# Sixteen instead of twelve feature tiles of a SwiGLU's gate and up projections by seven block products

## The chip, the cores and the metric

The kernel runs on one core of a Trainium2 chip, as one launch. The metric is the device time of that launch in microseconds (us), lower is better. Engines are named as in the profile: PE (TensorE, matrix products; PEld is its weight load), DVE (VectorE), ACT (ScalarE), POOL (GpSimd) and SP, whose queue issues nearly all the DMAs here.

## The reference

A decoder trunk of two layers over 512 tokens with 1024 features, all in float32. Each layer is a SwiGLU half step, a mixing step with three attention branches, and a second SwiGLU half step. There are therefore four SwiGLU sub-layers, and the change touches these alone:

```python
def _swiglu(t, w_gate, w_up, w_down):
    return (jax.nn.silu(t @ w_gate) * (t @ w_up)) @ w_down

for l in range(DEPTH):                      # DEPTH = 2
    f = _swiglu(_rmsnorm(h, ffn1_pre_g[l]), ffn1_w_gate[l], ffn1_w_up[l], ffn1_w_down[l])
    h = h + 0.5 * _rmsnorm(f, ffn1_post_g[l])
    ...                                     # mixing step
    f = _swiglu(_rmsnorm(h, ffn2_pre_g[l]), ffn2_w_gate[l], ffn2_w_up[l], ffn2_w_down[l])
    h = h + 0.5 * _rmsnorm(f, ffn2_post_g[l])
```

The hidden width D_FF is 2816, that is 22 tiles of 128 features.

## The kernel before, in words

**Products.** Every float32 operand is split in two parts, `h` (rounded by a cast on ACT) and `l` (the rest, a subtraction on DVE), and a product is three matmuls, h·h, h·l and l·h (`mm3`, lines 214 to 216). Weights come in pieces ("units") of 128 x 1024 values, 512 KB each: SP issues the load into one of two `raw` buffers, ACT casts it to `wh`, DVE subtracts to `wl`; there are four `wh` and four `wl` buffers. A queue of jobs `Q` runs PE work in a written order and asks for the units of the coming jobs ahead (four units, which is two products).

**The four sub-layers** are named a0, c0, a1, c1 (`ffn`, called four times). Each has 22 feature tiles for gate and up, computed in three ways:

- *Halved pair.* The first pair of tiles runs in two halves of the tokens, since the second half of the tokens is still being normalised (`halved`).
- *Plain pair.* Two feature tiles, all 512 tokens: gate (`gates`), then up (`ups`), 2 x 2 x 8 x 3 = 96 matmuls of 128x512.
- *Group.* Four feature tiles, token-major (`group`, `gate_up`). The product of a 2x2 block matrix of the activations (token halves by input halves) and a 2x2 block matrix of the weights (input halves by gate | up) is made by seven block products instead of eight, each 4 x 2 x 3 = 24 matmuls of 128x512. Their left factors are sums of activation blocks (`sums`: the tiles `r` and, split, `ag` 2 to 5); their right factors are sums of weight blocks, made on DVE in the tiles `kt` (`BlockUnit.load`). After a group, 16 transposes of 128x128 on PE turn the result feature-major (`feature_major`, tiles `th`), and ACT copies it to `hr`.

**Accumulators.** Each of the seven products accumulates in a pair of PSUM banks. `SUM` says in which of three sums product n lies, and a sum that is read out goes on being added to:

```python
SUM = (0, 1, 2, 0, 2, 0, 0)
ORDER = (0, 2, 3, 4, 5, 1, 6)        # the order in which the products run
```

The tag `mm` has four banks, that is two pairs. With sum 0 kept throughout, sum 1 and sum 2 take turns at the other pair. The read-out of products 0, 2 and 3 is a copy on ACT, of product 6 the silu on ACT, of 1, 4 and 5 an addition on DVE (line 744).

**Down.** Sixteen feature tiles go through two sets of seven block products with the down weights (`products`, `downs(0)` and `downs(1)`), the last six tiles through plain products (`down`).

**Order before, in each sub-layer.** Halved pair (tiles 0, 1); plain pair 14 with the three steps of `sums` beside it; groups at 2, 6, 10, each one's transposes after two products of the next; then plain pairs 16, 18 and 20 woven with the two sets of down products: gates 16, transposes, ups 16, down 0 2 3, gates 18, down 4 5 1 6, ups 18, down 0 2 3, gates 20, down 4 5 1 6, ups 20.

A scheduler turns what is written into a fixed order for each engine before anything runs, and adds the semaphores; each engine then takes its instructions in that order.

Of the kernel before, what the change touches and what calls it, by code (L numbers as in the profile page):

```python
# [17 lines left out]
P = 128  # L18
# [4 lines left out]
def kernel(  # L23
# [611 lines left out]
    W_H, W_U = 4.8, (8.0, 7.0, 7.0, 5.7)  # L635


    TG = (2, 6, 10)

    HR = ("q", "q", "o", "o", "o", "tri", "tri", "rs")  # L640
    ORDER = (0, 2, 3, 4, 5, 1, 6)

    def ffn(l, src, wg, wu, wd, dst, name, spare, aside=None):

# [8 lines left out]
        def hidden(f, pg, pu):  # L653
            s = tmp(f"s{name}_{f}")
            nc.scalar.activation(s[:], pg[:], AF.Silu)
            if f < NC * FC:
                nc.vector.tensor_tensor(pair(f)[:, f % 2], pu[:], s[:], ALU.mult)
                return
            nc.vector.tensor_tensor(s[:], pu[:], s[:], ALU.mult)
            t = blk("q" if f >= 20 else "o", f"hid{name}_{f}")  # L660
            hid[f] = t[:, 0], t[:, 1]
            split(*hid[f], s[:])
            if f == NF - 1:
                tc.keep_in_program_order(nc.scalar.preload_act_table_set("natural_log_exp_and_others"))

        def pair(f):

            i = f // 2
            if i not in hr:
                hr[i] = stile([P, 2, S], HR[i], f"hr{name}_{i}", F32)  # L670
            return hr[i]
# [47 lines left out]
            t = st["ag", n]  # L719
            return t[:, 0, k, c], t[:, 1, k, c]  # L720

        def gate_up(f, n, uns):
# [12 lines left out]
            if n in (0, 2, 3, 6):  # L735
                st["c", i, j] = stile([P, 2, S], "f", f"c{name}_{f}_{i}{j}", F32)
            t = st["c", i, j]
            for e in range(2):
                if n == 6:
                    nc.scalar.activation(t[:, e], pts[e][:], AF.Silu)  # L740
                elif n in (0, 2, 3):
                    nc.scalar.copy(t[:, e], pts[e][:])
                else:
                    nc.vector.tensor_tensor(t[:, e], t[:, e], pts[e][:], ALU.add)
            if n == 1:
                nc.scalar.activation(t[:], t[:], AF.Silu)
            if n in (1, 6):
                u = st["c", i, 1]
                nc.vector.tensor_tensor(u[:], u[:], t[:], ALU.mult)
                st["hid", f, i] = u  # L750

        def feature_major(f):

            for i in range(2):
                u = st.pop(("hid", f, i))
                for b in range(2):
                    f2 = f + 2 * b
                    pt = pbank("z", f"th{name}_{f2}_{i}")
                    for m in range(2):
                        for e in range(2):  # L760
                            nc.tensor.transpose(pt[:, (2 * m + e) * P:(2 * m + e + 1) * P],
                                                u[:, e, (2 * b + m) * P:(2 * b + m + 1) * P], ident[:])
                    yield 0.45
                    out_ = pt[:].rearrange("p (m q) -> p m q", m=2)
                    nc.scalar.copy(pair(f2)[:, :, HALVES[i]], out_)

        def group(f):

            keep = Keep(lambda i, k0: stile([P, 2, S], "v", f"kt{name}_{f}_{i}_{k0}", F32)[:])
            for n in ORDER:  # L770
# [4 lines left out]
                yield uns, (lambda n=n, uns=uns: gate_up(f, n, uns))  # L775
            yield [], lambda: feature_major(f)

        def park():
# [5 lines left out]
        def halved(f, ug, uu, half):  # L784
            if half == 0:
                st["p"] = [pbank("mm", f"p{x}{name}_{f + m}") for x in "gu" for m in range(2)]
            else:
                Q.hold, Q.pinned = False, True
                Q.load_ahead()
                Q.pinned = False  # L790
            c = HALVES[half]

            for uns, pts in ((ug, st["p"][:2]), (uu, st["p"][2:])):
                for low in (False, True):
                    for un in uns:
                        for k, (m, pt) in itertools.product(range(un.nk), enumerate(pts)):
                            kk, cols = un.k0 + k, slice(m * P, (m + 1) * P)
                            wh, wl = un.h[:, k, cols], un.l[:, k, cols]
                            ah, al = act(kk, c)
                            if low:  # L800
                                nc.tensor.matmul(pt[:, c], wh, al, start=False, stop=False, skip_group_check=True)
                                nc.tensor.matmul(pt[:, c], wl, ah, start=False, stop=kk == ND - 1, skip_group_check=True)
                            else:
                                nc.tensor.matmul(pt[:, c], wh, ah, start=kk == 0, stop=False, skip_group_check=True)
                            yield (1 + low) * S // 2 * PE_US
            if half == 1:
                for m in range(2):
                    hidden(f + m, st["p"][m], st["p"][2 + m])
# [94 lines left out]
        def some(n):  # L903
            for one in itertools.islice(todo, n):
                Q.add(*one)

        def plain(f, *n):

            ug = wpair(wg[l], ND, f * P, f"g{name}_{f}")
            uu = wpair(wu[l], ND, f * P, f"u{name}_{f}")  # L910
            Q.add(ug, lambda: gates(f, ug))
            some(n[0])
            behind()
            Q.add(uu, lambda: ups(f, uu))
            some(n[1])

        def turns(f):
            *jobs, turn = group(f)
            later.append(turn)
# [3 lines left out]
            Q.add([], lambda: iter(first_factor(ci, 0) or ()))  # L923
            return products(ci)

        ug, uu = wpair(wg[l], ND, 0, f"g{name}_0"), wpair(wu[l], ND, 0, f"u{name}_0")
# [3 lines left out]
        Q.add(ug + uu, lambda: halved(0, ug, uu, 0), src.ready((0, 1)))  # L930
        Q.add([], lambda: halved(0, ug, uu, 1), src.ready(range(NT)))
        Q.add([], lambda: iter(park() or ()))
        marks["first"] = len(Q.jobs)
        summed = sums()
        todo = iter([([], lambda: iter(next(summed) or ()))] * 3)
# [4 lines left out]
        some(1)  # L940
        todo = turns(2)
        some(7)
        for g in (6, 10):
# [6 lines left out]
        todo = iter(())  # L950
        pairs = [(wpair(wg[l], ND, f * P, f"g{name}_{f}"), wpair(wu[l], ND, f * P, f"u{name}_{f}")) for f in (16, 18)]
# [11 lines left out]
        xg, xu = wpair(wg[l], ND, 20 * P, f"g{name}_20"), wpair(wu[l], ND, 20 * P, f"u{name}_20")  # L963
# [4 lines left out]
        Q.add(xu, lambda: ups(20, xu))  # L968
        if aside is not None:
            Q.add([], lambda: iter((next(norm),)))  # L970
        if aside is not None:
# [777 lines left out]
```

## Time and profile before

| | |
|---|---|
| three timed runs | 2387.38, 2388.46, 2388.64 us; median 2388.46 |
| span of the profiled execution | 2385.9 us |
| PE busy | 2374.6 us (100% of the span), 11720 matmuls in the trace |
| PEld, DVE, ACT, POOL busy | 84%, 77%, 55%, 3% |
| DMA | 337.13 MB, 141 GB/s in the mean |

The span runs from the first to the last instruction of one profiled execution, for which only the span is recorded; the timed runs lie 1.5 to 2.7 us above it. "Busy" is the time in which at least one instruction of the engine ran. A matmul row of 390 ns is one matmul from its start to its modelled end; the next one starts long before that, so rates are read from differences of start times.

### The profile page before, as it was taken

Reading aid. Unit: us, or ns where it says so; the run is one execution under the profiler, and the core shown is the slowest. Engines: PE = TensorE matmul, PEld = TensorE weight load, DVE = VectorE, ACT = ScalarE, POOL = GpSimd, SP = SyncE. Lnnn points to the kernel's source line nnn. Section 1 sums busy time; section 2 is a strip of 40 time slices with the busy share of each in tenths; the row PEclk is TensorE's granted clock in tenths of the full one; section 3 lists DMA queues with packets and bytes.
Section 4 is the critical chain, followed back from the end, with each engine's and each line's share of the span. In section 5 each row is a group of like instructions: output and inputs, shape, how many; then the busy total and the mean of one; then the engine's idle time right before and its main releaser. Section 6 shows DMA issues by size and latency. Waiting matters only on the chain.

```text
span 2385.9 us, 30907 instructions
## 1 busy us (share of the span) xinstructions
PE 2374.6 (100%) x11720; PEld 2009.0 (84%) x11720; DVE 1834.2 (77%) x2525; ACT 1317.5 (55%) x2136; POOL 74.0 (3%) x130
## 2 busy tenths in 40 slices
PE   9999999999999999999999999999999999999998
PEld 8888888888888898888898888888888888988887
DVE  7786877678777687778787878776787766778686
ACT  5655555677655554554545554556675655455443
POOL 0000000001110000000000000000001100000000
PEclk9999999999999999999999999999999999999999
DMA  5554664222323445545544536532232244445453
GB/s 188 166 174 136 202 212 151 71 76 76 89 67 120 150 133 177 168 150 194 185 142 159 185 133 231 184 115 80 63 89 80 73 139 142 159 142 185 141 203 124
DMA packets 234265, 337.13 MB, mean 141 GB/s; under 512 B 10346, under 2 KB 133506, under 8 KB 233604
## 3 DMA queue, kind: packets, MB, share of 16 engines
q1 hardware_dynamic: 234016, 335.13, 43.2%
q8 instruction: 92, 1.51, 0.3%
q14 instruction: 57, 0.47, 0.1%
q0 software_dynamic: 96, 0.03, 0.0%
q10 hardware_dynamic: 4, 0.00, 0.0%
HBM read 320.44 MB, written 14.68 MB: 140 GB/s over the span
## 4 chain that ended last, share of the span: by engine, by line
PE 95%; DVE 2%; DMA 1%; ACT 1%; issue 0%; DVEq 0%; ACTq 0%
PE pg L216 4%; PE pg L214 4%; PE pg L215 4%; PE pta L214 3%; PE pta L216 3%; PE pta L215 3%; PE pdc L214 3%; PE pdc L215 3%; PE pdc L216 3%; PE ptc L215 3%; PE ptc L216 3%; PE ptc L214 3%; PE pda L215 3%; PE pda L216 3%; PE pda L214 3%; PE pb L214 2%
## 5 line engine op out<-in xcount | busy, mean ns | idle before, releaser
L214 PE MATMUL pg<-us_a,wh_wg 128*128 128x512 f32 x384 | 151.0, 393 | 0.0
L216 PE MATMUL pg<-us_a,wl_wg 128*128 128x512 f32 x384 | 149.7, 390 | 0.0
L215 PE MATMUL pg<-us_a,wh_wg 128*128 128x512 f32 x384 | 149.6, 390 | 0.0
L188 ACT CAST wh_tc<-ktc 128x1024 fp32r<-128x1024 f32 x60 | 62.6, 1052 | 83.3 <-DVE ktc L349 37.2
L188 ACT CAST wh_ta<-kta 128x1024 fp32r<-128x1024 f32 x60 | 62.6, 1052 | 80.9 <-DVE kta L349 34.5
L189 DVE TENSOR_TENSOR wl_tc<-ktc,wh_tc 128x1024 fp32r<-128x1024 f32 x60 | 72.8, 1222 | 25.1 <-ACT wh_tc L188 24.9
L189 DVE TENSOR_TENSOR wl_ta<-kta,wh_ta 128x1024 fp32r<-128x1024 f32 x60 | 72.8, 1222 | 24.2 <-ACT wh_ta L188 23.9
L215 PE MATMUL pda<-wl_da,aha 128*128 128x512 f32 x224 | 87.1, 389 | 0.0
L216 PE MATMUL pda<-wh_da,ala 128*128 128x512 f32 x224 | 87.1, 389 | 0.0
L214 PE MATMUL pda<-wh_da,aha 128*128 128x512 f32 x224 | 87.1, 389 | 0.0
L215 PE MATMUL pdc<-wl_dc,ahc 128*128 128x512 f32 x224 | 87.1, 389 | 0.0
L214 PE MATMUL pdc<-wh_dc,ahc 128*128 128x512 f32 x224 | 87.1, 389 | 0.0
L216 PE MATMUL pdc<-wh_dc,alc 128*128 128x512 f32 x224 | 87.1, 389 | 0.0
L216 PEld LDWEIGHTS pg<-us_a,wl_wg 128*128 128x128 f32 x384 | 72.1, 188 | 15.2
L215 PEld LDWEIGHTS pg<-us_a,wh_wg 128*128 128x128 f32 x384 | 72.2, 188 | 14.1
L214 PEld LDWEIGHTS pg<-us_a,wh_wg 128*128 128x128 f32 x384 | 72.1, 188 | 14.1
L192 DVE SCALAR_TENSOR_TENSOR wl_wg<-raw_wg,wh_wg 128x1024 fp32r<-128x1024 f32 x48 | 58.6, 1220 | 25.9 <-ACT wh_wg L191 25.3
L214 PE MATMUL pta<-wh_ta,aga 128*128 128x512 f32 x192 | 75.1, 391 | 0.0
L214 PE MATMUL ptc<-wh_tc,agc 128*128 128x512 f32 x192 | 75.1, 391 | 0.0
L215 PE MATMUL ptc<-wl_tc,agc 128*128 128x512 f32 x192 | 74.8, 390 | 0.2 <-DVE wl_tc L189 0.2
L216 PE MATMUL pta<-wh_ta,aga 128*128 128x512 f32 x192 | 74.7, 389 | 0.0
L216 PE MATMUL ptc<-wh_tc,agc 128*128 128x512 f32 x192 | 74.7, 389 | 0.0
(536 smaller groups left out, 7675.8 us busy)
## 6 DMA issues: line engine op xcount, KB each, us to landing
raw_da<-in_ffn_w_down_dram SPq DMA_DIRECT2D x58, 512.0 KB, 3.7
raw_dc<-in_ffn_w_down_dram SPq DMA_DIRECT2D x58, 512.0 KB, 3.3
raw_ta<-in_ffn_w_gate_dram SPq DMA_DIRECT2D x48, 512.0 KB, 3.7
raw_wg<-in_w_gate_dram SPq DMA_DIRECT2D x48, 512.0 KB, 3.6
raw_tc<-in_ffn_w_gate_dram SPq DMA_DIRECT2D x48, 512.0 KB, 3.7
kta<-in_ffn_w_up_dram SPq DMA_DIRECT2D x24, 512.0 KB, 4.9
raw_wo<-in_w_out_dram SPq DMA_DIRECT2D x24, 512.0 KB, 3.3
ktc<-in_ffn_w_up_dram SPq DMA_DIRECT2D x24, 512.0 KB, 4.9
```

Of the source, the lines that this page charges most:

```text
L188: both = [nc.scalar.copy(h_ap, src)]
L189: make = lambda: nc.vector.tensor_tensor(l_ap, src, h_ap.bitcast(F32), ALU.subtract)
L192: make = lambda: nc.vector.scalar_tensor_tensor(l_ap, src, scale, h_ap.bitcast(F32), ALU.mult, ALU.subtract)
L214: nc.tensor.matmul(pt, lh, rh, start=start, stop=False, skip_group_check=free)
L215: nc.tensor.matmul(pt, lh, rl, start=False, stop=False, skip_group_check=free)
L216: nc.tensor.matmul(pt, ll, rh, start=False, stop=stop, skip_group_check=free)
```

## The change

Sixteen feature tiles go through groups, at 0, 4, 8 and 12, one after the other (before: twelve, at 2, 6 and 10). The halved pair is now tiles 16 and 17, and two plain pairs are left, 18 and 20, both woven with the down products. The plain pair behind the halved pair is gone, so that the first group stands there. This first group runs its products in the order `FIRST` = 0, 1, ..., 6; products 0 and 1 need no sums of activations. The first step of `sums` is traced in the second half of the halved pair, the second ahead of product 0, the third ahead of product 1. The hidden tiles 16 and 17 are split at once for the plain down products. The transposes of the last group take `mm` banks in place of `z` banks. Buffers of `hr` are taken from other tags.

The new order of a sub-layer: halved pair 16; sums; products 0 and 1 of the first group with the last step of the sums between them; its products 2 to 6; groups 4, 8, 12; down 0 2; gates 18; the last transposes; down 3 4 5; ups 18; down 1 6; down 0 2 3 of the second set; gates 20; down 4 5 1 6; ups 20.

```diff
-    TG = (2, 6, 10)
-    HR = ("q", "q", "o", "o", "o", "tri", "tri", "rs")
+    TG = (0, 4, 8, 12)
+    EARLY = NC * FC
+    HR = ("o", "o", "o", "o", "o", "o", "tri", "tri")
     ORDER = (0, 2, 3, 4, 5, 1, 6)
+    FIRST = (0, 1, 2, 3, 4, 5, 6)
...
         def hidden(f, pg, pu):
             s = tmp(f"s{name}_{f}")
             nc.scalar.activation(s[:], pg[:], AF.Silu)
-            if f < NC * FC:
-                nc.vector.tensor_tensor(pair(f)[:, f % 2], pu[:], s[:], ALU.mult)
-                return
             nc.vector.tensor_tensor(s[:], pu[:], s[:], ALU.mult)
-            t = blk("q" if f >= 20 else "o", f"hid{name}_{f}")
+            t = blk("q" if f < EARLY + 2 else "o", f"hid{name}_{f}")
...
-            if n in (1, 6):
+            if n == 6 or n == last_of_top:
                 u = st["c", i, 1]
-                nc.vector.tensor_tensor(u[:], u[:], t[:], ALU.mult)
+                nc.vector.tensor_tensor(u[:], u[:], st["c", i, 0][:], ALU.mult)
...
-                    pt = pbank("z", f"th{name}_{f2}_{i}")
+                    pt = pbank("mm" if f == TG[-1] else "z", f"th{name}_{f2}_{i}")
...
         def group(f):
+            order = FIRST if f == TG[0] else ORDER
+            top = max((1, 4), key=order.index)
...
         def halved(f, ug, uu, half):
...
                 Q.load_ahead()
                 Q.pinned = False
+                next(summed)
...
-        plain(14, 1, 1)
+        add_sums()
+        todo = turns(TG[0])
+        some(1)
+        add_sums()
+        some(7)
...
-        pairs = [... for f in (16, 18)]
-        Q.add(pairs[0][0], lambda: gates(16, pairs[0][0]))
+        pairs = [... for f in (18, 20)]
+        todo = downs(0)
+        some(2)
+        Q.add(pairs[0][0], lambda: gates(18, pairs[0][0]))
         behind()
-        todo = downs(0)
-        Q.add(pairs[0][1], lambda: ups(16, pairs[0][1]))
         some(3)
-        Q.add(pairs[1][0], lambda: gates(18, pairs[1][0]))
+        Q.add(pairs[0][1], lambda: ups(18, pairs[0][1]))
         some(7)
-        Q.add(pairs[1][1], lambda: ups(18, pairs[1][1]))
         todo = downs(1)
         some(3)
...
-        Q.add(xg, lambda: gates(20, xg))
+        Q.add(pairs[1][0], lambda: gates(20, pairs[1][0]))
         some(4)
...
```

More of the change, by code (lines that the diff above doesn't have):

```diff
@@ L720, in input_block, with gate_up @@
             return t[:, 0, k, c], t[:, 1, k, c]
-        def gate_up(f, n, uns):
+        def gate_up(f, n, uns, last_of_top):
             if n in (0, 1, 2):
@@ L767, in group @@
         def group(f):
+            order = FIRST if f == TG[0] else ORDER
+            top = max((1, 4), key=order.index)
             keep = Keep(lambda i, k0: stile([P, 2, S], "v", f"kt{name}_{f}_{i}_{k0}", F32)[:])
-            for n in ORDER:
+            for n in order:
                 uns = []
@@ L905, in some @@
                 Q.add(*one)
[L907 to L915, printed above, removed]
         def turns(f):
@@ L924, in downs @@
             return products(ci)
-        ug, uu = wpair(wg[l], ND, 0, f"g{name}_0"), wpair(wu[l], ND, 0, f"u{name}_0")
+        ug, uu = (wpair(w[l], ND, EARLY * P, f"{x}{name}_{EARLY}") for x, w in (("g", wg), ("u", wu)))
         marks["early"] = ug + uu
@@ L929, in ffn @@
             un.tags = place
-        Q.add(ug + uu, lambda: halved(0, ug, uu, 0), src.ready((0, 1)))
-        Q.add([], lambda: halved(0, ug, uu, 1), src.ready(range(NT)))
+        summed = sums()
+        add_sums = lambda: Q.add([], lambda: iter(next(summed) or ()))
+        Q.add(ug + uu, lambda: halved(EARLY, ug, uu, 0), src.ready((0, 1)))
+        Q.add([], lambda: halved(EARLY, ug, uu, 1), src.ready(range(NT)))
         Q.add([], lambda: iter(park() or ()))
         marks["first"] = len(Q.jobs)
-        summed = sums()
-        todo = iter([([], lambda: iter(next(summed) or ()))] * 3)
-        plain(14, 1, 1)
+        add_sums()
[3 more added lines that the diff above has]
+        some(7)
         if name == "a0":
@@ L939, in ffn @@
             Q.add([], lambda: iter(mem_stats() or ()))
[L940 to L943, printed above, removed]
+        for g in TG[1:]:
             todo = turns(g)
@@ L949, in ffn @@
             later[:] = over
[L950 to L952 removed]
+        pairs = [(wpair(wg[l], ND, f * P, f"g{name}_{f}"), wpair(wu[l], ND, f * P, f"u{name}_{f}")) for f in (18, 20)]
+        todo = downs(0)
+        some(2)
+        Q.add(pairs[0][0], lambda: gates(18, pairs[0][0]))
         behind()
[L954 to L955 removed]
         some(3)
[L957 removed]
+        Q.add(pairs[0][1], lambda: ups(18, pairs[0][1]))
         some(7)
[L959 removed]
         todo = downs(1)
@@ L967, in ffn @@
             Q.add([], lambda: iter((next(norm),)))
-        Q.add(xu, lambda: ups(20, xu))
+        Q.add(pairs[1][1], lambda: ups(20, pairs[1][1]))
         if aside is not None:
```

3 lines of the change are left out of this document (1 added, 2 removed).

## The prediction

> **What bounds the kernel now.** I read the page's table of engines first, then PE's list of waits, then PE's transposes on the chain that ended last, then the order in time of DVE and PE where the first group starts.
>
> ```profile
> PE 2374.6 (100%) x11720; PEld 2009.0 (84%) x11720; DVE 1834.2 (77%) x2525; ACT 1317.5 (55%) x2136; POOL 74.0 (3%) x130
> ```
> ```profile
> engine line waited for: us in total, times, longest us
> PE pts L1186 <- ACT ts L1217: 1.5, 2, 0.7
> ...
> PE ptc L215 <- DVE wl_tc L189: 0.2, 1, 0.2
> ```
>
> PE is busy for the whole span and waits for others for some 4 us in all (the longest cause is 1.5 us). So the time is the number of PE's instructions times their pace, plus whatever new idle time PE gets. The pace comes from the chain, where the 16 transposes behind a group of a0 stand as one piece each (start, duration):
>
> ```profile
> 109.50 1.75 PE tha L761 x16
> 149.34 1.75 PE tha L761 x16
> 189.19 1.75 PE tha L761 x16
> ```
>
> From one to the next are 39.84 us, one whole group: 7 x 24 = 168 matmuls and 16 transposes of 1.75 us. A matmul of 128x512 thus takes (39.84 - 1.75) / 168 = 0.2267 us of PE.
>
> **PE's work, part by part.** Per sub-layer four feature tiles move from two plain pairs (192 matmuls, 43.53 us) to a group (39.84 us): 3.69 us less. The built program of the changed kernel has 96 matmuls of 128x512 fewer and 64 transposes more over the four sub-layers. Term 1: -4 x 3.69 = **-14.8 us**. This holds only while nothing makes PE wait.
>
> **The start of the first group.** Before, the plain pair 14 (96 matmuls, 21.8 us of PE) stood between the halved pair and the first group, and under it DVE made the sums of activations. Now products 0 and 1 alone stand there: 48 x 0.2267 = 10.9 us. Then comes product 2, and it needs two banks. Of the four `mm` banks product 0's pair is kept (sum 0 goes on), so product 2 must take product 1's pair, which is free only when DVE has added product 1 out of it. With `ORDER` the corresponding read-out had a whole product (5) to hide under; with `FIRST` it has none. In the changed kernel's fixed order DVE comes to these two additions late: in c0, a1 and c1 it has, from the first sum of activations to the second addition, 24 instructions of 128x1024 (12 for the sums and their splits, 8 weight splits of products 0 to 3, 4 weight sums) and 6 of 128x512 (two silu products, their two splits, the two additions). PE's order even puts the first 9 matmuls of product 3 ahead of product 2, and these wait for product 3's first weight split, the 23rd of the 24.
>
> The prices, from DVE's order in time (start, duration, instruction), c0 of the kernel before:
>
> ```profile
> 870.07 1.21 DVE L679 TENSOR_TENSOR rc<-us_b 128x1024 f32<-128x1024 f32 x1
> 871.20 2.35 DVE L189 TENSOR_TENSOR wl_gc<-raw_gc,wh_gc 128x1024 fp32r<-128x1024 f32 x2
> 873.47 2.35 DVE L679 TENSOR_TENSOR rc<-us_b 128x1024 f32<-128x1024 f32 x2
> 875.74 1.22 DVE L685 TENSOR_TENSOR rc<-rc,rc 128x1024 f32<-128x1024 f32 x1
> ...
> 882.07 1.28 DVE L657 TENSOR_TENSOR hrc<-puc,sc 128x512 f32<-128x512 f32 x2
> 883.27 3.73 DVE L685 TENSOR_TENSOR rc<-rc,rc 128x1024 f32<-128x1024 f32 x3
> ```
>
> Back to back, an instruction of 128x1024 takes (875.74 - 870.07) / 5 = 1.134 us and one of 128x512 (883.27 - 882.07) / 2 = 0.60 us. The list costs 24 x 1.134 + 6 x 0.60 = 30.8 us. It cannot begin earlier than now, since it begins with the first sum, for which the last activations must be there. The anchors, DVE's first sum and PE's first matmul behind the halved pair (which tells when the halved pair is done), c0's sum being above:
>
> ```profile
> 880.50 0.40 PE L214 MATMUL pgc<-us_b,wh_gc 128*128 128x512 f32 x1
> ```
> ```profile
> 1212.68 1.21 DVE L679 TENSOR_TENSOR ra<-us_c 128x1024 f32<-128x1024 f32 x1
> ```
> ```profile
> 1223.12 0.40 PE L214 MATMUL pga<-us_c,wh_ga 128*128 128x512 f32 x1
> ```
> ```profile
> 2052.48 1.22 DVE L679 TENSOR_TENSOR rc<-us_b 128x1024 f32<-128x1024 f32 x1
> ```
> ```profile
> 2062.91 0.40 PE L214 MATMUL pgc<-us_b,wh_gc 128*128 128x512 f32 x1
> ```
> ```profile
> 34.73 2.35 DVE L189 TENSOR_TENSOR wl_ga<-raw_ga,wh_ga 128x1024 fp32r<-128x1024 f32 x2
> ```
> ```profile
> 37.92 0.40 PE L214 MATMUL pga<-us_x,wh_ga 128*128 128x512 f32 x1
> ```
>
> c0: PE ends product 1 at 880.50 + 10.9 = 891.4; DVE frees the banks at 870.07 + 30.8 = 900.9. PE sits idle from 891.4 to about 898.5 (four half and 23 wide instructions: 28.5 us after 870.07), does the 9 matmuls of product 3 (2.0 us, work that is needed anyway) and starts product 2 at 900.9. Lost: 900.9 - 891.4 - 2.0 = 7.5 us. a1: 1243.5 - 1234.0 - 2.0 = 7.5. c1: 2083.3 - 2073.8 - 2.0 = 7.5. In a0 some sums are done ahead of 34.73 already; from there 19 wide and 6 half instructions remain, 25.1 us: 59.8 - 48.8 - 2.0 = 9.0. Term 2: **+31.5 us**. This has DVE without any wait. In the same place of the kernel before it waits a little, for a cast of a weight that had to be loaded:
>
> ```profile
> 2062.36 1.23 DVE L189 TENSOR_TENSOR wl_uc<-raw_uc,wh_uc 128x1024 fp32r<-128x1024 f32 x1 [0.73 <-ACT wh_uc L188]
> ...
> 2078.45 1.23 DVE L337 TENSOR_TENSOR ktc<-ktc,raw_tc 128x1024 f32<-128x1024 f32 x1 [2.30 <-DMA raw_tc<-in_ffn_w_gate_dram]
> ```
>
> Such waits now lengthen PE's. Bounds 0 to 2.3 us per sub-layer; the second wait came when DVE was well ahead, so I stay near the first row: 0.5 each. Term 3: **+2 us**.
>
> **The clock behind that idle time.** PE's idle stretch of 7.1 us (8.7 in a0) is longer than any within the kernel now. What an idle PE does to its clock is seen at the end only, after the last matmul (stretch, then its length, busy times of PE, PEld, DVE, ACT, POOL, then granted clock):
>
> ```profile
> 2378.43 0.28 PE L216 MATMUL pdc<-wh_dc,hidc 128*128 128x256 f32 x1
> ```
> ```profile
> 2383.00:2384.00 1.00, 0.00 (x0) 0.00 (x0) 0.00 (x0) 0.00 (x0) 0.00 (x0) 0.94 0.98 347
> 2384.00:2385.00 1.00, 0.00 (x0) 0.00 (x0) 0.00 (x0) 0.00 (x0) 0.00 (x0) 0.50 0.11 38
> ```
>
> PE's last matmul ends at 2378.7, and from 2383.9 the granted clock is 0.50: it was halved after 5.2 us of idleness. All four idle stretches are longer, so PE should come back at half pace. How long that lasts is shown at the start, where the transposes ran slowly up to 11.7 us (min/median/max):
>
> ```profile
> L1649 PE MATMUL utx<-ident,fx x16: 273/421/422, 8.5 to 11.7; 128*128 128x128 f32 x16
> ```
>
> PE had begun at about 1.3 us then, so at worst some 10 us go at half pace: 5 us lost per sub-layer. At best nothing is lost. The work there was thin and broken, here it is dense, so I go below the middle: 2 us each. Term 4: **+8 us**. The Trainium skill ("TensorE: Matmul & The Clock Gate", Part 1) speaks against the change here: it has the clock halved after an idle window of about 3.4 us and full again about 4 us into sustained matmuls. By that page each stretch would lose about 2 us and the sum stay as it is; the fall after 5.2 us agrees with it, the slow start does not, or not with 4 us.
>
> **Smaller new waits.** In `FIRST`, products 5 and 6 stand together in sum 0, so 6 waits for 5's read-out by DVE (with `ORDER`, product 1 lay between). Price: a matmul's tail of 0.39 - 0.23 = 0.16 us and one addition,
>
> ```profile
> 929.01 0.69 DVE L744 TENSOR_TENSOR cc<-cc,ptc 128x512 f32<-128x512 f32 x1 [0.40 <-PE ptc L216]
> ```
>
> 0.85 us, less two matmuls of the next group that PE's order pulls ahead (0.45): 0.4, with the signalling 0.5 (0 to 1.5). Term 5: **+2 us**. The last group's four transpose tiles share `mm` with gates 18; the fourth waits for ACT to copy the first, behind a cast:
>
> ```profile
> L188 ACT CAST wh_tc<-ktc 128x1024 fp32r<-128x1024 f32 x60 | 62.6, 1052 | 83.3 <-DVE ktc L349 37.2 <-PE puc L215 16.6 <-DVE ktc L340 8.9
> ...
> L765 ACT COPY hrc<-thc 128x512 f32<-128x512 f32 x24 | 12.3, 602 | 0.0
> ```
>
> That is 0 to 1.65 us; I take 0.5, as two transpose tiles run meanwhile. Term 6: **+2 us**. In the down stage one plain pair fewer gives DVE shelter. Now, in a0 (same columns as above):
>
> ```profile
> 190.00:329.00 139.00, 139.00 (x627) 115.51 (x626) 112.52 (x133) 70.02 (x95) 0.52 (x1) 1.00 0.53 178
> ```
>
> A plain pair costs DVE 4 x 1.134 + 4 x 0.60 = 6.9 us and PE 21.8; without one, DVE has 105.6 of PE's 117.2 us, 90%, still less than all. But between ups 18 and gates 20 five products now follow each other (before at most four): 27.2 us of PE and, at (105.6 - 13.8) / 14 = 6.6 us each, 32.8 us of DVE. The gap of 5.6 us is met by what DVE has done ahead, two products' weight splits, 4 x 1.134 = 4.5 us, and more of the left factors. Bounds 0 to 5.6 per sub-layer, taken 0.5. Term 7: **+2 us**.
>
> At nothing I cost: 24 more loads on SP (12.6 MB more than 337; the queue of the first group's loads waits on DVE's splits, and term 3 has that), ACT's additional casts (ACT is 55% busy, and what it does late DVE does late: term 3), and the groups in a row, since three in a row run without idleness now, 39.84 us each.
>
> **Sum.** -14.8 + 31.5 + 2 + 8 + 2 + 2 + 2 = +32.7 us. Against the profiled span 2385.9 that is 2418.6; the timed median lies 2.6 us above the span, so 2388.46 + 32.7 = **2421.2 us**.
>
> **Rivals.**
>
> *A, no clock loss.* The stretches occur but PE comes back at full pace, and the small waits hide: 2388.46 - 14.8 + 31.5 = 2405.2. Against it stands the fall after 5.2 us. Chance 0.15; half-way cases are in my range.
>
> *B, DVE is short in the down stage too.* If little is done ahead there, the full gap of 5.6 us is lost in each sub-layer in place of 0.5, or the loads hold DVE by 2.3 us in place of 0.5: +20 or +7. With the first, 2441. Against: the total is only 90%, and no PE wait stands in that stage now. Chance 0.12.
>
> *C, faster.* The first group starts without a stretch: term 1 with terms 5 to 7 is -8.8, so 2379.7. It decides at one point: the two additions must be done by the end of product 1, 9.5 us earlier than I reckon, so 8 to 9 of the 24 wide instructions must lie behind them or ahead of the first sum. For it: the sums start one step earlier in the written order, and products 0 and 1 need none of them. Against: an engine takes its instructions in their fixed order, and none of the 24 stands elsewhere. Chance 0.05; between that and slower, within the 0.2% (4.8 us) that a measurement here can tell from no change, 0.02.
>
> My case has 0.66, with a range of its own of 2411 to 2432 (the clock at 0 to 5 us per stretch, partly offset, and the waits at 0 to 1). Eight in ten need part of A and of B: 2404 to 2435. Slower by over 0.2%: 0.93.
>
> **What would show it.** In the changed kernel's list of PE's waits, four waits of 7 to 9 us for product 3's `wl_t` split and some tenths for the sum tile `c`, at the first group of each sub-layer; DVE without a gap in the 30 us before; a granted clock of 0.5 for some microseconds behind each. Groups 4, 8 and 12 at 39.84 us each show term 1. If PE's idle time is under 10 us in all, term 2 is wrong, and C holds; if PE idles in the down stage, B does.

## The result, and the profile after

| | before | changed |
|---|---|---|
| median of the timed runs | 2388.34 us (2387.38 to 2388.64) | 2431.9 us (2427.58 to 2432.74) |
| ratio | | 1.0178 (1.0164 to 1.0193) |
| span of the profiled execution | 2385.9 us | 2425.7 us |

The change costs 43.6 us; 32.7 were forecast (2421.2, range 2404 to 2435). The profiled execution is the fastest of the four of the changed kernel, 39.8 us above the one of before; the trace is set against these 39.8, and the section on the hardware says what may make the rest.

First the table of engines of the changed kernel, and rows of PE's list of waits (total, times, longest):

```profile
PE 2378.2 (98%) x11688; PEld 2001.0 (82%) x11688; DVE 1911.1 (79%) x2597; ACT 1363.0 (56%) x2198; POOL 74.1 (3%) x130
```
```profile
PE pta L214 <- ACT wh_ta L188: 11.2, 2, 6.6
PE ptc L214 <- ACT wh_tc L188: 9.8, 2, 4.9
PE pta L215 <- DVE wl_ta L189: 5.3, 4, 1.7
PE ptc L215 <- DVE wl_tc L189: 3.8, 3, 1.5
PE pta L214 <- ACT ca L741: 1.7, 2, 1.0
...
PE pda L215 <- DVE wl_da L189: 0.9, 2, 0.8
PE thc L760 <- ACT hrc L764: 0.6, 1, 0.6
PE pga L216 <- DVE wl_ga L189: 0.5, 2, 0.3
...
PE tha L760 <- ACT hra L764: 0.2, 1, 0.2
```

PE is busy for 3.6 us longer than before, although it has 14.8 us less to do, and it waits for some 39 us in all where it waited for 4. The two upper rows are four waits, one in each sub-layer. PE's order in time in c0 shows one (start, duration, instruction, then the idle time ahead of it and who ended it); the first row is the first matmul of the first group, the last two are the transposes of groups 0 and 4:

```profile
893.93 0.40 PE L214 MATMUL ptc<-wh_tc,us_b 128*128 128x512 f32 x1
...
905.22 0.39 PE L216 MATMUL ptc<-wh_tc,us_b 128*128 128x512 f32 x1
910.52 1.22 PE L214 MATMUL ptc<-wh_tc,agc 128*128 128x512 f32 x2 [4.91 <-ACT wh_tc L188]
913.23 0.80 PE L215 MATMUL ptc<-wl_tc,agc 128*128 128x512 f32 x1 [1.49 <-DVE wl_tc L189]
913.83 0.63 PE L216 MATMUL ptc<-wh_tc,agc 128*128 128x512 f32 x1
...
916.38 0.63 PE L214 MATMUL ptc<-wh_tc,agc 128*128 128x512 f32 x1
...
953.97 1.91 PE L760 MATMUL thc<-ident,cc 128*128 128x128 f32 x16
...
993.82 1.91 PE L760 MATMUL thc<-ident,cc 128*128 128x128 f32 x16
```

Products 0 and 1 end at 905.6. Then PE stands until 910.52, takes the first two of product 3's nine matmuls, waits again, and comes back at half pace: rows of 0.63 us, one every 0.43 us. The tenth matmul behind the gap, at 916.38, is the first of product 2. From the start of the first group to its transposes lie 216 matmuls, 48.97 us at full pace; here they take 953.97 - 893.93 = 60.04, in a0, a1 and c1 60.53, 59.20 and 59.50. From group 0's transposes to group 4's it is 39.85 us again.

DVE's order in time over the same stretch: its first sum, the one split that waited, the two splits of product 3's weights, the two additions of product 1:

```profile
883.50 1.22 DVE L678 TENSOR_TENSOR rc<-us_b 128x1024 f32<-128x1024 f32 x1
...
893.65 1.23 DVE L189 TENSOR_TENSOR wl_tc<-raw_tc,wh_tc 128x1024 fp32r<-128x1024 f32 x1 [0.86 <-ACT wh_tc L188]
...
911.96 2.35 DVE L189 TENSOR_TENSOR wl_tc<-ktc,wh_tc 128x1024 fp32r<-128x1024 f32 x2
914.23 1.28 DVE L743 TENSOR_TENSOR cc<-cc,ptc 128x512 f32<-128x512 f32 x2
```

From 883.50 to 915.51 are 32.0 us: the 30.8 reckoned and one wait of 0.9.

### The profile page after: what moved, and what is told of

Read it like the earlier page. It is cut to its first block, busy times and chain, and to the rows that moved or that the text cites. A ratio compares the mean times of both kernels' runs of the same rounds, so it can differ in the third digit from the quotient of the medians.

```text
span 2425.7 us, 31080 instructions
## 1 busy us (share of the span) xinstructions
PE 2378.2 (98%) x11688; PEld 2001.0 (82%) x11688; DVE 1911.1 (79%) x2597; ACT 1363.0 (56%) x2198; POOL 74.1 (3%) x130
## 4 chain that ended last, share of the span: by engine, by line
PE 79%; DVE 9%; DMA 5%; ACT 3%; issue 3%; POOL 0%; SPq 0%; DVEq 0%; ACTq 0%; POOLq 0%
PE ptc L215 4%; PE ptc L216 4%; PE ptc L214 4%; PE pg L216 3%; PE pg L214 3%; PE pg L215 3%; PE pta L215 3%; PE pta L216 3%; PE pta L214 3%; PE pdc L214 2%; PE pdc L215 2%; PE pdc L216 2%; PE pb L214 2%; PE pb L215 2%; PE pb L216 2%
## 5 line engine op out<-in xcount | busy, mean ns | idle before, releaser
L188 ACT CAST wh_ta<-kta 128x1024 fp32r<-128x1024 f32 x80 | 83.2, 1052 | 99.5 <-DVE kta L349 31.8
L188 ACT CAST wh_tc<-ktc 128x1024 fp32r<-128x1024 f32 x80 | 83.2, 1051 | 93.4 <-DVE ktc L349 28.9
L189 DVE TENSOR_TENSOR wl_tc<-ktc,wh_tc 128x1024 fp32r<-128x1024 f32 x80 | 96.8, 1222 | 35.3 <-ACT wh_tc L188 35.1
L189 DVE TENSOR_TENSOR wl_ta<-kta,wh_ta 128x1024 fp32r<-128x1024 f32 x80 | 96.9, 1223 | 32.0 <-ACT wh_ta L188 31.6
L214 PE MATMUL pta<-wh_ta,aga 128*128 128x512 f32 x256 | 102.0, 400 | 12.9 <-ACT wh_ta L188 11.2
L214 PE MATMUL ptc<-wh_tc,agc 128*128 128x512 f32 x256 | 102.1, 400 | 9.8 <-ACT wh_tc L188 9.8
L215 PE MATMUL pta<-wl_ta,aga 128*128 128x512 f32 x256 | 101.6, 397 | 4.6 <-DVE wl_ta L189 4.6
L215 PE MATMUL ptc<-wl_tc,agc 128*128 128x512 f32 x256 | 101.8, 398 | 3.0 <-DVE wl_tc L189 3.0
L216 PE MATMUL ptc<-wh_tc,agc 128*128 128x512 f32 x256 | 101.4, 396 | 0.0
L216 PE MATMUL pta<-wh_ta,aga 128*128 128x512 f32 x256 | 101.1, 395 | 0.0
```

Of the source, the lines that this page charges most:

```text
L188: both = [nc.scalar.copy(h_ap, src)]
L189: make = lambda: nc.vector.tensor_tensor(l_ap, src, h_ap.bitcast(F32), ALU.subtract)
L214: nc.tensor.matmul(pt, lh, rh, start=start, stop=False, skip_group_check=free)
L215: nc.tensor.matmul(pt, lh, rl, start=False, stop=False, skip_group_check=free)
L216: nc.tensor.matmul(pt, ll, rh, start=False, stop=stop, skip_group_check=free)
```

## The experiments

The short diffs are against the changed kernel; what a kernel takes over from an earlier one is named, not shown again. Theory Q is the prediction's: DVE's queue ahead of product 2's banks. For each kernel the period of each sub-layer (from the end of its halved pair to the next one's, or between two other equal points) is compared with the kernel before, in us, where the table has an entry; a0 and a1 hold the mixing steps too, and -3.7 is the most that a sub-layer can gain. The periods are those of one profiled execution, which can lie some us from the median (e3_busy's is 5.7 below it):

| kernel | time | ratio to before | a0 | c0 | a1 | c1 |
|---|---|---|---|---|---|---|
| changed | 2431.9 | 1.0178 | +13.4 | +8.0 | +10.3 | +8.2 |
| e9_place | 2429.9 | 1.0176 | +14.2 | +9.2 | +9.5 | +9.8 |
| e3_busy | 2421.0 | 1.0132 | | | | |
| e5_order_pool | 2418.7 | 1.0127 | | | | |
| e2_order | 2404.8 | 1.0069 | | | | |
| e6_sums, e7_stats | 2404.8, 2403.6 | 1.0070, 1.0065 | | | | |
| e1_bank | 2403.0 | 1.0061 | +10.0 | -0.2 | +2.8 | +2.8 |
| e8_pair | 2402.4 | 1.0060 | +7.1 | +3.5 | +6.4 | -1.0 |
| e11_early | 2397.6 | 1.0041 | +7.2 | -0.7 | +2.5 | +0.6 |
| e10_nosums | 2392.7 | 1.0019 | +9.2 | -3.1 | +1.4 | -0.6 |
| e13_tables | 2392.4 | 1.0017 | +1.6 | -0.9 | +4.0 | +0.4 |
| e12_nofactors | 2387.4 | 0.9996 | +1.8 | -0.7 | +2.6 | -3.7 |

The intervals of the ratios reach 0.0009 to 0.0017 to either side.

**e1_bank.** Product 2 in other banks.

```diff
-                st["gb", SUM[n]] = [pbank("mm", f"pt{name}_{f}_{n}_{e}") for e in range(2)]
+                st["gb", SUM[n]] = [pbank("z" if f == TG[0] and n == 2 else "mm", f"pt{name}_{f}_{n}_{e}") for e in range(2)]
```

> The changed kernel, but product 2 of each first group gets its two banks from z, which is free there, in place of mm. Theory Q (the queue of DVE and the two mm banks: product 2 has to wait for the two additions that stand at the end of 30.8 us of DVE): product 2 follows product 1 at once, since its weight splits are the 16th and 17th wide instruction; product 3 then still waits for the 23rd, 28.5 us after the first sum, while PE is ready 27 us after it: about 3 us lost per sub-layer in place of 10 to 11 (4.5 in a0), and no halved clock, since the stretch stays under 5.2 us. Time 2431.9 - 28 = 2404 (2398 to 2410). Theory L (loads and casts: PE's list of waits names ACT's casts of the weights of product 3; the casts wait for loads): the banks do not matter, product 3 or 2 still begins 5 to 7 us late behind product 1 and the time is 2425 or more.

2403.0, as theory Q had it. PE's order now is 0, 1, 2, 3, product 2 follows at once, and one long wait is left in c0; the clock is halved in one place only, a0's second group. The first row is that wait; the second has, from the start of the group on, the length and the engines' busy times (PE, PEld, DVE, ACT, POOL):

```profile
909.35 0.50 PE L215 MATMUL ptc<-wl_tc,agc 128*128 128x512 f32 x1 [1.73 <-DVE wl_tc L189]
```
```profile
890.50:932.00 41.50, 39.48 (x175) 31.50 (x174) 39.46 (x40) 22.40 (x28) 0.00 (x0) 1.00 0.55 179
```

Theory L fails: with the same loads and casts the time falls by 29 us. The casts that PE's list names for the changed kernel were late because they stood behind DVE: in c0 the two weight sums of product 3 run from 907.42 to 909.77, and ACT casts from 909.43, busy until then with left factors that another sum of DVE had released at 907.5. The second row shows what remains: DVE is busy for 39.5 of 41.5 us.

**e2_order.** The first group in the order of the others.

```diff
-    FIRST = (0, 1, 2, 3, 4, 5, 6)
+    FIRST = ORDER
```

> The changed kernel with the first group of each sub-layer in the order 0 2 3 4 5 1 6 of the other groups. Theory Q: product 1's banks are no longer in the way, and the read-outs of products 2 and 4 have product 5 to hide under; DVE then has 17 wide and 4 half instructions up to product 3's weights (21.7 us after the first sum, PE is ready 21.3 us after it) and 23 wide up to product 4's left factor (28.5 us against 27.2): about 2 us lost per sub-layer, no halved clock, no wait between products 5 and 6. Time 2431.9 - 34 = 2398 (2392 to 2405). Theory L: the same number of loads and casts stands ahead of products 2 and 3 as before, a stretch of 5 to 7 us stays, and the time is 2420 or more.

2404.8: the long wait and the halved clock are gone, which theory L excluded. It is 7 us more than forecast: the stall turned into many waits of 0.5 to 2.6 us for splits and for read-outs.

**e3_busy.** Twenty matmuls of 128x512 more in PE's gap, into a bank of `z`.

```diff
-        some(7)
+        some(1)
+        Q.add([], keep_busy)
+        some(6)
```

> The changed kernel with 20 extra matmuls of 128x512 (4.5 us, their result is not used) behind product 1 of each first group, in a free bank, so that PE is idle for under 1 us there in place of 5. If the halved clock is what adds some 2.2 us per sub-layer behind the stretch (theory Q with its clock term), the granted clock stays at 1.00 and the time falls by 4 x 2.2 = 9 to 2423, although PE has 80 matmuls more. If the slow matmuls behind the stretch are due to something else (weights arriving late), the time stays at 2432.

2421.0, 11 us faster with 80 matmuls more. The windows around the gap in c0 (length, busy times, then the granted clock, third from the end) stay at 1.00, and a1 is at full clock too:

```profile
903.00:908.00 5.00, 4.71 (x21) 3.49 (x20) 5.00 (x6) 3.44 (x4) 0.00 (x0) 1.00 0.10 37
908.00:916.00 8.00, 6.05 (x27) 4.74 (x26) 4.53 (x5) 2.32 (x3) 0.00 (x0) 1.00 0.01 2
```

In a0 and c1 it is not, so the full clock came in two places of the four:

```profile
55.18:62.01 6.83, 5.35 (x12) 3.76 (x13) 6.17 (x7) 2.21 (x3) 0.00 (x0) 0.50 0.01 1
2103.18:2106.59 3.41, 3.41 (x9) 2.63 (x8) 1.73 (x3) 1.06 (x1) 0.00 (x0) 0.50 0.00 0
```

Of the changed kernel's 34.1 us at half clock 10.2 are left in this execution. The cleanest price is that of the two places at full clock: from the start of the first group to its transposes c0 takes 56.89 us in place of 60.04 and a1 57.09 in place of 59.20 (in c0 DVE's additions, too, come 0.7 us sooner after the start of the group).

**e5_order_pool.** e2_order, and four of the eight sums of activations on POOL (in `whole` and `block_sum`).

```diff
-            nc.vector.tensor_tensor(t[:], src.us[j][:, :, 0, HALVES[i]].bitcast(F32),
+            eng = nc.gpsimd if i == 0 else nc.vector
+            eng.tensor_tensor(t[:], src.us[j][:, :, 0, HALVES[i]].bitcast(F32),
...
-            nc.vector.tensor_tensor(r, *(st["r", x // 10, x % 10][:] for x in (a, b)), op)
+            eng = nc.gpsimd if n in (4, 5) else nc.vector
+            eng.tensor_tensor(r, *(st["r", x // 10, x % 10][:] for x in (a, b)), op)
```

> As e2_order, and four of the eight sums of activations per sub-layer (the two of the first token half, and those for products 4 and 5) run on POOL, which is idle there, in place of DVE. Theory Q: DVE has 16 wide instructions instead of 17 ahead of product 3 and 21 instead of 23 ahead of product 4's left factor; what is left of the waits of e2_order (about 2 us per sub-layer) goes, if POOL takes under 5 us for a sum of 128x1024: time 2391 (2386 to 2400). If POOL is slower than that, or slows DVE by sharing, product 3 waits for POOL's sum and the time is above e2_order's.

2418.7, 14 us slower than e2_order, by the reason named last. The orders in time of DVE and POOL in c0:

```profile
889.27 3.28 DVE L337 TENSOR_TENSOR ktc<-ktc,raw_tc 128x1024 f32<-128x1024 f32 x1 [0.34 <-DMA raw_tc<-in_ffn_w_gate_dram]
...
895.89 3.42 DVE L337 TENSOR_TENSOR ktc<-ktc,raw_tc 128x1024 f32<-128x1024 f32 x1
...
900.43 2.21 DVE L189 TENSOR_TENSOR wl_tc<-ktc,wh_tc 128x1024 fp32r<-128x1024 f32 x1
```
```profile
889.07 2.40 POOL L686 TENSOR_TENSOR rc<-rc,rc 128x1024 f32<-128x1024 f32 x1 [8.29 <-DVE rc L686]
894.91 3.31 POOL L679 TENSOR_TENSOR rc<-us_b 128x1024 f32<-128x1024 f32 x1 [3.44 <-DVE agc L189]
898.30 3.26 POOL L686 TENSOR_TENSOR rc<-rc,rc 128x1024 f32<-128x1024 f32 x1
```

An addition takes POOL 2.4 to 3.3 us, and a DVE instruction that meets it takes 2.2 to 3.4 us in place of 1.2. Behind PE's waits for these the clock is halved again: it is at 0.50 for 6.8 us in each of c0, a1 and c1, and nowhere there in e2_order. So the 14 us are the price of the sharing and of the clock together.

**e6_sums.** e1_bank, and the last four wide instructions of the sums behind product 1.

```diff
         todo = turns(TG[0])
-        some(1)
+        some(2)
         add_sums()
```

> As e1_bank (product 2 of the first group in the free banks; 2403.0), and the third step of the sums of activations, which only products 4 and 5 need, stands behind product 1 in place of product 0. Four wide instructions of DVE then come behind the weight splits of product 3, which end 25.7 us after the first sum, while PE is ready for them 26.7 us after it. Theory Q: the 1.7 us that PE waits there in each of c0, a1, c1 go, with the tail of each some 2.5 us per sub-layer: 2403 - 10 = 2393 (2388 to 2399). If what holds product 3 is not DVE's order but the casts or loads of its weights, the time stays at 2403.

2404.8 (2402.5 to 2406.7): no gain over e1_bank, a miss. In c0, a1 and c1 the wait for product 3 did go, as forecast, but each got a new one at the next tight place, product 6 behind 5 and the early transposes. PE's order in time in c0:

```profile
926.64 0.73 PE L214 MATMUL ptc<-wh_tc,us_b 128*128 128x512 f32 x2 [1.21 <-ACT wh_tc L188]
...
928.03 1.09 PE L760 MATMUL thc<-ident,cc 128*128 128x128 f32 x8 [0.66 <-DVE cc L748]
```

To the transposes of group 4 e1_bank loses 3.3, 4.2 and 4.2 us in c0, a1 and c1, e6_sums 3.5, 5.0 and 3.2. I read what is lost as a debt of DVE, which a new order moves and does not pay; e10 and e11 test this.

**e7_stats.** e6_sums, and a0's statistics of the memory rows (`mem_stats`) behind the last group.

> As e6_sums, and in a0 the statistics of the memory rows (two squares with sums and four table loads on ACT, in the trace beside a0's second group) come behind the last group. In the changed kernel PE waits there 1.7 us for ACT's copies out of PSUM and 1.7 us for a weight split behind a late cast; if ACT's queue is the cause, these some 4 us of a0 go: 2389 (2384 to 2395), if they do not come back in the down stage. If it is a debt of DVE from the first group, e6_sums has removed them already and this kernel equals e6_sums.

2403.6: the waits went from the second group (its loss fell by some 6 us) to the transposes of the last group and the first down products. Moving ACT's work did not help; e13 shortens it.

**e8_pair.** The plain pair 18 back behind the halved pair (with the sums, and `ORDER` for the first group), only the pair 20 in the down stage.

```diff
+        todo = iter([([], lambda: iter(next(summed) or ()))] * 3)
...
+        Q.add(eg, lambda: gates(EARLY + 2, eg))
         some(1)
+        Q.add(eu, lambda: ups(EARLY + 2, eu))
+        some(1)
...
         todo = downs(0)
         some(2)
-        Q.add(pairs[0][0], lambda: gates(18, pairs[0][0]))
         behind()
-        some(3)
-        Q.add(pairs[0][1], lambda: ups(18, pairs[0][1]))
+        some(2)
+        Q.add(xg, lambda: gates(20, xg))
         some(7)
         todo = downs(1)
-        some(3)
+        some(2)
+        Q.add(xu, lambda: ups(20, xu))
...
```

> The changed kernel's sixteen tiles in groups, but the plain pair 18 stands behind the halved pair, with the sums beside it and the first group in the order of the others, as in the kernel before; only the pair 20 is left among the down products. Theory Q: no stretch at the first group, no halved clock; the gain of 14.8 us is paid against the down stage alone. There DVE needs 14 x 6.6 + 6.9 = 99 us against PE's 14 x 5.44 + 21.8 = 98, so DVE is short by 1 us and by what its order loses: 1 to 4 us per sub-layer. Time 2388.2 - 14.8 + 8 = 2381 (2377 to 2390). The rival that four groups in a row or the thin cover of the down stage cost most of the loss gives 2400 or more.

2402.4, a miss by 21 us. The first groups lose 0 to 3 us at full clock, as forecast (the longest wait there is one of 2.4 us in a0); the down stage loses what the groups gain and more. From its list of waits, and its windows for the down stage of c0:

```profile
PE utc L619 <- DVE fc L609: 3.3, 3, 1.3
PE pta L215 <- DVE wl_ta L189: 3.3, 4, 1.5
PE pda L215 <- DVE wl_da L189: 2.9, 4, 0.8
...
PE pda L216 <- DVE ala L189: 2.3, 4, 0.8
```
```profile
1078.00:1215.00 137.00, 133.68 (x631) 110.20 (x630) 119.43 (x159) 74.55 (x118) 0.00 (x0) 1.00 0.53 177
```

PE now waits for DVE's splits of down weights and left factors and, at the end of a sub-layer, for the next one's normalised tokens (`fc`). My sum of 99 against 98 us of DVE and PE allowed 1 to 4 us for DVE's order, which was too little: DVE is busy for 119 of these 137 us and is late all the same. I take it that it cannot work ahead by more than its buffers hold, and that the normalisation behind the last down products adds to it; no run takes these two apart.

**e9_place.** The kernel before, with one part of the change: the first group behind the halved pair, in the order 0 to 6, and the plain pair 14 behind the last group.

> The kernel before with one part of the change: the first group stands directly behind the halved pair (order 0 to 6, sums moved as in the change), the plain pair 14 comes behind the last group; still twelve tiles in groups and three pairs among or ahead of the down products. Theory Q: the whole loss comes with this place, and the gain of 14.8 us is missing: 2388.2 + 47 (43 at the four starts, 4 in a0's second group) = 2435 (2428 to 2446). The rival that the four groups in a row and the down stage with two pairs make the loss: 2388 to 2400.

2429.9, 42 us above before. Its waits at the first groups:

```profile
PE pta L214 <- ACT wh_ta L188: 10.8, 2, 7.4
PE ptc L214 <- ACT wh_tc L188: 7.8, 2, 4.0
```

The new place, with its order, is enough for a loss of this size. But the changed kernel has 14.8 us of PE work less than this one and is 2 us slower by the medians, 3 us faster by the profiled executions: the rest of the change eats most of its gain.

**e10_nosums.** e1_bank without `whole(0, 0)`, `whole(0, 1)` and the four `block_sum`s.

> As e1_bank, and six of the eight DVE instructions that make the sums of activations per sub-layer are left out (the left factors of products 2 to 5 are split from two of the plain blocks; so a part of the computation is missing). This takes 6 x 1.134 = 6.8 us of DVE out of each first group, and no load, cast or matmul. If the 3 to 4 us that e1_bank and e6_sums still lose per sub-layer are DVE's debt, which moves but stays when its order is changed, they go, with some of a0's: 2403 - 14 = 2389 (2384 to 2394). If they come from loads, casts or banks, the time stays at 2400 or more.

2392.7, in the range: 10 of the 14 us. The start of c0 takes 49.24 us, against 48.97 with no loss at all, and c0 gains 3.1 us. a0 still loses 9.2.

**e11_early.** e1_bank, and two sums ahead of the second half of the halved pair.

```diff
-            whole(0, 0)
...
-            whole(0, 1)
...
+        Q.add([], lambda: iter((whole(0, 0), whole(0, 1)) and ()))
         Q.add([], lambda: halved(EARLY, ug, uu, 1), src.ready(range(NT)))
```

> As e1_bank, and the two sums over the first half of the tokens are made before the second half of the halved pair, while DVE waits for ACT's statistics of the last tokens. That takes 2 x 1.134 = 2.3 us of DVE out of the stretch that starts with the first sum. If DVE's debt is the price, the time falls by about 2 us in each of c0, a1, c1 and hardly in a0, where the tokens are there early: 2403 - 6 = 2397 (2393 to 2402). If the two sums delay the last tokens by as much as they save, it stays at 2403.

2397.6: the time is as forecast, the places are so only in part. To the transposes of group 4 c0, a1 and c1 take 1.4, 2.9 and 1.6 us less than in e1_bank, but a0 also takes 2.4 less, where hardly anything was forecast; and of the periods in the table, c0 and a1 keep only 0.5 and 0.3. Still, of the arrangements that compute everything and move DVE's work, this is the one that makes its debt smaller: the two sums went to a place where DVE stood idle (2.1 us ahead of its last normalisation step in c0 of the changed kernel).

**e12_nofactors.** e8_pair without the later sums of hidden blocks.

```diff
-                elif n == 3:
-                    nc.vector.tensor_tensor(s, s, a(0, 0), ALU.subtract)
-                elif n == 4:
-                    nc.vector.tensor_tensor(s, a(0, 1), s, ALU.subtract)
-                elif n == 5:
-                    nc.vector.tensor_tensor(s, a(0, 0), a(1, 0), ALU.subtract)
```

> As e8_pair (plain pair 18 behind the halved pair, only pair 20 among the down products; 2402.4), and the three later sums of hidden blocks per set of down products are left out (12 instructions of 128x512, 7.2 us of DVE per sub-layer; a part of the computation is missing), with loads, casts and matmuls as they were. If DVE is what the down stage lacks without its second pair, the some 7 us per sub-layer that e8_pair lost against its PE work go: 2402 - 24 = 2378 (2374 to 2388). If it is the loads or the order, the time stays at 2398 or more.

2387.4: 15 us of the 24 that I gave to DVE come back, at the upper end of the range; the other 9 stay open. c1 gains the full 3.7; a0 and a1 stay above before, with waits for splits and casts of down weights.

**e13_tables.** e11_early, and one table load for the statistics of both memory rows (in `mem_stats`).

```diff
-            nc.scalar.activation(ss[:, 1:2], ss[:, 0:1], AF.Ln)
-            nc.scalar.activation(ss[:, 1:2], ss[:, 1:2], AF.Exp, scale=-0.5)
+        tc.keep_in_program_order(nc.scalar.preload_act_table_set("natural_log_exp_and_others"))
+        for t in range(MT):
+            ss = mem_rstd[:, t]
+            tc.keep_in_program_order(nc.scalar.activation(ss[:, 1:2], ss[:, 0:1], AF.Ln))
+            tc.keep_in_program_order(nc.scalar.activation(ss[:, 1:2], ss[:, 1:2], AF.Exp, scale=-0.5))
```

> As e11_early (2397.6), and in a0 the statistics of the memory rows load ACT's function table once for both rows in place of four times (3 loads of 1.28 us less on ACT, in the stretch where PE waits 2.2 and 1.0 us for ACT's copies out of PSUM in a0's second group). If ACT's queue there is the cause of these waits, they and their tails go: 2397.6 - 3.5 = 2394 (2391.5 to 2396.5). If it is a debt of DVE in a0, the time stays at 2397 to 2398.

2392.4, 5.2 us faster, 1.7 more than forecast: in e11_early these waits had halved the clock too, as PE's order in time shows by its row of 0.80 us:

```profile
101.25 0.50 PE L214 MATMUL pta<-wh_ta,aga 128*128 128x512 f32 x1 [2.25 <-ACT ca L739]
...
103.24 0.80 PE L214 MATMUL pta<-wh_ta,aga 128*128 128x512 f32 x1 [1.02 <-ACT ca L739]
```

That cost e11_early 1.6 us of PE's work (3.1 us at half clock). Its trace has the clock halved for 3.4 us in a0's first group as well, which e13's has not, so the surplus of 1.7 us has two possible sources. The changed kernel's orders in time of ACT and PE show the cause of the waits, a0's second group:

```profile
104.45 1.28 ACT L1055 ACT_TABLE_LOAD   x1
...
105.86 0.57 ACT L741 COPY ca<-pta 128x512 f32<-128x512 f32 x1
106.44 1.28 ACT L1056 ACT_TABLE_LOAD   x1
...
107.85 0.57 ACT L741 COPY ca<-pta 128x512 f32<-128x512 f32 x1
```
```profile
106.48 0.50 PE L214 MATMUL pta<-wh_ta,aga 128*128 128x512 f32 x1 [0.67 <-ACT ca L741]
...
108.47 0.51 PE L214 MATMUL pta<-wh_ta,aga 128*128 128x512 f32 x1 [1.02 <-ACT ca L741]
```

Product 4 waits for each of the two copies of product 2, and each stands behind a table load. In the kernel before these loads cost PE nothing. With this, the changed arrangement is still 0.17% (0.08 to 0.26) slower than the kernel before; no arrangement of the sixteen tiles here that computes the whole reference beats it.

## Why the prediction was right, by its steps

**The bound and term 1** (-14.8). PE sets the time, and groups 4, 8 and 12 follow each other at 39.85 us. That the gain exists is shown where DVE was relieved, though by leaving out work that the result needs: c0 of e10 gains 3.1 us, c1 of e12 3.7.

**Terms 2 to 5, the start of the first group** (31.5 + 2 + 8 + 2 = 43.5). Measured against 48.97 us (49.19 in a0, as before): 11.3, 11.1, 10.2 and 10.5, in all 43.2. DVE's queue has nearly the reckoned length (32.0, 31.1 and 31.4 us in c0, a1 and c1, against 30.8), the order of PE is the one named, and e1, e2 and e9 show that the banks and the place are the cause. Two details were otherwise. The forecast had one wait of 7 to 9 us for product 3's split; there are two, of 4.6 to 6.6 us for its cast and then of 1.5 for the split, since its first two matmuls use only the cast half. And in c0 the additions end at 915.51, but product 2 begins only at 916.38, since product 3's nine matmuls ran at half pace. PE's list names casts on ACT; that row tells who came last, and not who was late.

**Term 4, the clock** (8, and rival A without it). The clock was halved in all four places, but not on the ground given: the idle stretches were to be longer than 5.2 us, and only a0's is (6.6; the others are 4.9, 4.6 and 4.9). PE had work for 4.4, 6.5, 5.0 and 4.5 us of the halved time, so at most half of that is lost, 10.2 us; it is less, since product 3's slow matmuls ran in part while product 2 would have waited for the additions anyway (in all four places it begins only 0.9 us behind their end). e3's two places at full clock are 3.2 and 2.1 us faster. So rival A is out, the size of term 4 is right within these bounds, and it is luck that the four terms together fit to 0.3 us.

**Terms 6 and 7, and what I costed at nothing** (4): mis-sized. The trace has 39.8 + 14.8 - 43.2 = 11.4 us there. Of these 4.3 are a0's second group (its transposes come 44.11 us after the first's, not 39.85): the table loads, as e13 shows; I had costed ACT's work at nothing. That the slack of ACT and DVE covered them before is my reading. The other 7.1 lie in and behind the down stages; the list of waits names 2.2 of them (down splits 0.9, gates 20 0.5, transposes 0.8), each with a tail, and I did not find all of the rest. **Rival B** is false for the changed kernel at its full price, and true as soon as the second pair goes too (e8).

**Rival C** failed at its one point: the additions came 10 us behind the end of product 1.

## What to carry to other kernels

Before a kernel's main engine is given less work, count what the engine that feeds it has to do between the event that starts it and the release that the main engine waits for; 14.8 us of PE were bought here with 77 us of DVE (1911.1 against 1834.2 busy), at places where DVE had no slack. Here a new use of the banks (e1) or a new order (e2) removed the long stall and the halved clock behind it, some 28 us; what was left then only moved with a further new order (e6, and e8 with the covering pair moved back, end within 2 us of e1). Only work taken out of that queue (e10, e12), or moved into a gap where the engine idles (e11), paid some of it. And a wait is read twice: the row names the last releaser, the queue behind the releaser names the cause.

## What the runs showed of the hardware

**The clock moves on a grid.** Windows of the changed kernel, granted clock third from the end; the first three are c0, the last two a1:

```profile
908.00:908.50 0.50, 0.00 (x0) 0.00 (x0) 0.50 (x1) 0.50 (x2) 0.00 (x0) 0.77 0.00 0
918.00:918.50 0.50, 0.50 (x2) 0.33 (x1) 0.00 (x0) 0.00 (x0) 0.00 (x0) 0.50 0.00 0
918.50:919.00 0.50, 0.50 (x4) 0.38 (x3) 0.00 (x0) 0.00 (x0) 0.00 (x0) 0.99 0.00 0
...
1259.00:1260.00 1.00, 0.00 (x0) 0.00 (x0) 1.00 (x2) 1.00 (x2) 0.00 (x0) 0.92 0.00 0
1266.00:1267.00 1.00, 1.00 (x4) 0.81 (x3) 0.00 (x0) 0.26 (x1) 0.00 (x0) 0.67 0.00 0
```

From the share of each window at half clock, it is halved from 908.27 to 918.51 (10.24 us) in c0 and from 1259.84 to 1266.66 (6.82 us) in a1; a0 has 10.2 (from 51.52), c1 6.8 (from 2109.76). The four falls lie 856.75, 351.57 and 849.92 us apart, which is 251, 103 and 249 times 3.413 us: they stand on one grid. The Trainium skill ("TensorE: Matmul & The Clock Gate", Part 1) tells of an activity window of 3413 ns that runs freely; 6.82 and 10.24 are two and three of these, which agrees.

It fell 2.2 to 4.3 us after PE's last matmul, not 5.2 as at the end of the kernel before, so shorter gaps suffice than I had taken. What decides, by these traces, is how much of a gap lies in one window of the grid. In all traces of this case, from 20 us after the start on, the clock fell 35 times (14 of them at the kernel's end), each time behind a window in which PE was idle for 56% or more (once 45%), and no window at full clock that was followed by another was idle for more than 53%. So a gap of 1.95 us in c1 of e3_busy, which lies within one window, was followed by half clock, and PE's wait of 2.39 us in a0 of e8_pair, which the grid cuts in two, by full clock (its two windows, with PE busy for 1.71 and 2.72 of 3.41 us):

```profile
69.43:72.84 3.41, 1.71 (x8) 1.09 (x6) 2.02 (x5) 3.37 (x5) 0.00 (x0) 1.00 0.00 0
72.84:76.25 3.41, 2.72 (x12) 2.24 (x13) 0.85 (x4) 3.38 (x6) 0.00 (x0) 1.00 0.00 0
```

The phase of that window is not the kernel's: the other three timed runs have spans of 2429.6 to 2430.9 at a mean clock of 0.991 to 0.992, the profiled one 2425.7 at 0.993. At 0.991 some 2430 x 0.009 / 0.5 = 44 us are halved, at 0.993 some 34, and half of the difference is 5 us. That is the size of the difference between the profiled execution and the median; no trace of the slower runs shows it.

**POOL and DVE exclude each other** here (e5): in the rows shown, each DVE instruction that starts while POOL adds ends 1.1 us after POOL's addition, as if it had only then begun (892.55 after 891.47, 899.31 after 898.22, 902.64 after 901.56). Four additions moved to POOL cost 14 us, the clock's part included. The Trainium skill ("SBUF — State Buffer", "SBUF: two separate sides") states an exclusive lock between a DVE instruction with two SBUF inputs and a GpSimd one that reads SBUF; the rows above agree.
